# Turning 128x128 squares on TensorE as two half tiles that land in two PSUM banks

## The chip, the cores and the metric

The kernel runs on one core of a Trainium2 chip. The metric is the device time of one execution in microseconds (us). TensorE (PE in the profile) multiplies, VectorE (DVE), ScalarE (ACT) and GpSimd (POOL) do the elementwise work, SyncE (SP) issues the transfers. PE writes its results to PSUM, which has eight banks of 2 KB for each of 128 partitions (512 float32 numbers); the other engines read them from there.

## What is computed

One layer of a streaming encoder for one sequence of 1024 tokens of width 1024 in float32, with 16 meta tokens ahead of it. A mixer of two branches and an MLP, each with a normalization ahead and a residual around it:

```python
def hybrid_mixer(u, ...):                       # u = rmsnorm(h, norm_mix)
    z = u @ w_in                                # split into a, q, k, v, r, lr, ga, gb
    y_a = pooled(a) @ w_pool_mix ... @ w_pool_out
    o = gla_chunked(q, k, v, log_a)             # chunks of 64 tokens, 4 heads, keys 64 wide, values 128
    o = rmsnorm(o, gla_norm) * silu(r)
    y_b = o @ w_gla_out
    m = sigmoid(ga) * y_a + sigmoid(gb) * y_b
    return m @ w_out

h = h + hybrid_mixer(rmsnorm(h, norm_mix), ...)
h = h + squared_relu_mlp(rmsnorm(h, norm_ffn), w_ff1, w_ff2)
return rmsnorm(h, norm_final)[:, 16:]           # the meta tokens are dropped
```

Within a chunk, `gla_chunked` forms scores of queries and keys with a decay between them; across chunks it carries a state of 64x128 numbers for each head.

## The kernel before, in words

**Products.** A float32 product is made as three products of two-part numbers, hi times hi, lo times hi and hi times lo (`mm3`, lines 285 to 287). A step of `mm3` is three instructions of 128x128 weights that move up to 512 columns. ACT makes each hi part by rounding, DVE each lo part by subtracting. The projections and both MLP layers use seven products in place of eight on 2x2 blocks.

**Turning.** A product needs the contracted index on the partitions, so activations that stand token by token are turned. That is done on PE by `pe.transpose`: a 128x128 square of the activation is loaded as the weights, an identity matrix is moved through, and the turned square comes out in PSUM. Four squares fill a bank. The places are:

- line 525, `turn` of the first stage: eight tiles of 128 tokens of the normalized input (`us`), 8 squares each in a bank of the pool `ms` and one of `sc`. Its readers are `keep` (L531, ACT), `hi` (L538, ACT) and `lo` (L541, DVE);
- line 278: the 16 meta tokens, 8 pieces of 16x128;
- line 1417, in `across`, the part of the linear attention that carries the state: the keys `gi`, twice 8 squares, read by ACT (L1418);
- line 1461, later in `across`: the normalized output `on`, 32 squares, read by DVE (L1462);
- line 1589, `turn_tile`: the normalized input of the MLP (`u`), eight tiles of 8 squares. Six of them stand between the products of `out_tile` (the product with `w_out`, second half of its columns, `ch` = 1), two between the first products of the MLP's first layer, `ff1`. Readers are L1594, L221 and L222 for four of the tiles and L1598 to L1609 for the other four.

All in all 176 squares of 128x128, in 21 visits: 20 of 8 squares and one, in `across`, of 16. Ahead and behind of a visit stand ordinary products.

**Order.** PE's order is the program's own. In the first stage the orders of ACT, DVE and SP are written out as well (a list named ORDER_1). Elsewhere a scheduler orders ACT, DVE and SP by when it thinks that data are there. So a change of the PSUM pools can reorder DVE and ACT.

**PSUM.** The eight banks are split into pools by `banks(...)`, and the split changes from stage to stage: a product takes a bank of its pool when the earlier tenant has been read. `two(name)` takes a pair of neighbouring banks as one tile. In the linear attention before the change there are three `mm` banks for the products that fill in (`yb_block` among them, whose bank is read by L1388), one pair `m2`, one pair `sc` and one bank `ms`.

The tile positions of the profile read "64*64 64x64": a tile of 64 rows and 64 columns of the array that moves 64 columns. Such tiles exist before the change in `scores` (L1188), `across` (L1423, L1437, L1447).

Of the kernel before, what the change touches and what calls it, by code (L numbers as in the profile page):

```python
# [122 lines left out]
def kernel(  # L123
# [26 lines left out]
    banks(sc=1, mm=3, ms=3)  # L150
# [110 lines left out]
    turn_n = [0]  # L261

    def transposed(u, half, at, tags=("ms",), to=None):
        rows = u.shape[0]
        th, tl = (t[half] for t in to or (TH, TL))
        if rows == P:
            for j in range(2):
                turn_n[0] += 1
                b = bank(tags[turn_n[0] % len(tags)]).rearrange("p (a b) -> p a b", a=4)
                for i in range(4):  # L270
                    pe.transpose(b[:, i], u[:, (4 * j + i) * P : (4 * j + i + 1) * P], ident)
                split_from_psum(th[:, 4 * j : 4 * j + 4, at : at + P], tl[:, 4 * j : 4 * j + 4, at : at + P], b)
                c = half * HALF + at - OFF[half]
                act.activation(S["xr"][:, 4 * j : 4 * j + 4, c : c + P], b, ACT.Copy)
        else:
            b = bank("ms")[:, : 8 * rows].rearrange("p (a b) -> p a b", a=8)
            for i in range(8):
                pe.transpose(b[:, i], u[:, i * P : (i + 1) * P], ident[:rows, :rows])
            split_from_psum(th[:, :, at : at + rows], tl[:, :, at : at + rows], b)
# [165 lines left out]
    def first_stage(xs, us, xm, um, lrraw):  # L445
# [75 lines left out]
        def turn(t, j):  # L521
            turn_n[0] += 1
            b = turned[t, j] = bank(("ms", "sc")[turn_n[0] % 2]).rearrange("p (a b) -> p a b", a=4)
            for i in range(4):
                pe.transpose(b[:, i], x_out(t)[:, (4 * j + i) * P : (4 * j + i + 1) * P], ident)

        def kept(t, j):
            return xr[:, 4 * j : 4 * j + 4, t * P : (t + 1) * P]
# [4 lines left out]
        def part(a, t, j):  # L533
            half, at = tok(t)
            return a[half][:, 4 * j : 4 * j + 4, at : at + P]
# [640 lines left out]
    def part(i):  # L1176
        return slice(i * CH, (i + 1) * CH)

    def scores(kk, qq):
# [5 lines left out]
        for j in range(4):  # L1185
            for e, u in ((0, 0), (1, 1), (1, 0), (0, 1)):
# [93 lines left out]
    def gla_open():  # L1280
# [22 lines left out]
        banks(keep=1, mm=3, m2=1, ms=1)  # L1303
# [100 lines left out]
    def across(p, half):  # L1404
# [10 lines left out]
        b = quad(bank("ms") if p == 0 else wide2()[:, 0])  # L1415
        for j in range(4):
            pe.transpose(b[:, j], kl[:, j * P : (j + 1) * P], ident)
# [514 lines left out]
```

## Time and profile before

| | us |
|---|---|
| median of 3 runs (lowest to highest) | 1202.58 (1202.22 to 1203.32) |
| profiled execution | 1203.16 |
| its span, first to last instruction | 1201.4 |
| PE busy | 1187.1 |
| DVE busy | 854.1 |
| ACT busy | 578.7 |

The mean clock that TensorE was granted is 0.998. From 0 to about 60 us the span holds the first stage, to 180 the first products of the projections, to 380 the pairs of projections with the scores between them, to 480 the part of the linear attention that carries the state with the filling products, to 580 the product with `w_out`, and then the MLP.

A row of the timeline reads: start in us, duration in us, engine, line, operation, output<-inputs by the program's names, the tile of the array where it is a PE instruction, the moved form and the count of merged instructions, and in brackets the idle time ahead of it with what ended it. Durations of PE instructions overlap, since they are pipelined, so the pace is read from start to start. A row of the waits reads: the waiting engine, tile and line, `<-`, what ended the wait, and then the total in us, the count, and the longest.

### The profile page before, as it was taken

To read this page: it belongs to the slowest core of one execution; us is meant where nothing else is said; L and a number is where in the kernel's file an instruction comes from. 1 tells how busy PE (TensorE), PEld (TensorE's weight loads), DVE (VectorE), ACT (ScalarE), POOL (GpSimd) and SP (SyncE) were. 2 spreads that over 40 slices of the span, in tenths; PEclk is the share of its full clock that TensorE was granted. 3 is DMA by queue.
4 is the path that set the end of the run, shared out by engine and by line. 5 is a ranking of instruction groups with operands and counts; after the bars stand their busy time and mean duration, and the time that the engine had idled before them with its cause. 6 is when DMAs were issued, how large, how long until landed. Compare 5 with 4: busy or idle time off the path is not lost.

```text
span 1201.4 us, 18340 instructions
## 1 busy us (share of the span) xinstructions
PE 1187.1 (99%) x6775; PEld 987.7 (82%) x6775; DVE 854.1 (71%) x1392; ACT 578.7 (48%) x1006; POOL 101.5 (8%) x121
## 2 busy tenths in 40 slices
PE   9999999999999999999999999999999999999997
PEld 7999888777778887888788888888888888888886
DVE  6679557575676669617886767667675887887686
ACT  7566544444455224205754545545454444445554
POOL 0224232333220000000000000000000000000000
PEclk9999999999999999999999999999999999999999
DMA  8232633434358877801264444444389963333532
GB/s 246 68 89 80 182 109 119 144 117 141 124 178 269 304 229 269 268 26 71 88 198 136 158 147 162 148 158 161 128 282 324 336 222 97 97 97 92 172 97 88
DMA packets 151001, 192.79 MB, mean 160 GB/s; under 512 B 12088, under 2 KB 85616, under 8 KB 150912
## 3 DMA queue, kind: packets, MB, share of 16 engines
q1 hardware_dynamic: 150752, 191.56, 49.6%
q8 instruction: 53, 0.87, 0.3%
q14 instruction: 36, 0.29, 0.1%
q10 hardware_dynamic: 160, 0.07, 0.0%
HBM read 128.66 MB, written 62.93 MB: 159 GB/s over the span
## 4 chain that ended last, share of the span: by engine, by line
PE 68%; DVE 3%; issue 1%; DMA 1%; ACT 1%; SPq 0%; DVEq 0%
PE b_oa L287 5%; PE b_oa L286 5%; PE b_oa L285 5%; PE b_y L285 4%; PE b_y L287 4%; PE b_y L286 4%; PE b_mm L285 4%; PE b_mm L287 4%; PE b_mm L286 4%; PE b_ob L287 4%; PE b_ob L286 4%; PE b_ob L285 4%; PE b_z L286 3%; PE b_z L285 3%; PE b_z L287 3%; PE b_sc L285 2%
## 5 line engine op out<-in xcount | busy, mean ns | idle before, releaser
L285 PE MATMUL b_z<-th,w1h 128*128 128x512 f32 x240 | 94.3, 393 | 0.0
L286 PE MATMUL b_z<-tl,w1h 128*128 128x512 f32 x240 | 93.5, 390 | 0.4 <-DVE tl L1601 0.4
L287 PE MATMUL b_z<-th,w1l 128*128 128x512 f32 x240 | 93.5, 390 | 0.0
L285 PE MATMUL b_sc<-th,w1h 128*128 128x512 f32 (+1 forms) x232 | 89.8, 387 | 0.6 <-ACT u2p L1715 0.6
L286 PE MATMUL b_sc<-tl,w1h 128*128 128x512 f32 (+1 forms) x232 | 89.2, 385 | 0.0
L967 ACT ACTIVATE w1h<-raw 128x512 fp32r<-128x512 f32 x103 | 64.0, 622 | 52.4 <-PE b_y L286 23.0
L287 PE MATMUL b_sc<-th,w1l 128*128 128x512 f32 (+1 forms) x232 | 88.9, 383 | 0.0
L967 ACT ACTIVATE w1h<-fs 128x512 fp32r<-128x512 f32 x81 | 51.1, 631 | 66.3 <-PE b_y L286 34.8
L968 DVE TENSOR_TENSOR w1l<-raw,w1h 128x512 fp32r<-128x512 f32 x103 | 70.7, 688 | 15.7 <-ACT w1h L967 15.7
L968 DVE TENSOR_TENSOR w1l<-fs,w1h 128x512 fp32r<-128x512 f32 x81 | 56.2, 693 | 21.6 <-ACT w1h L967 21.6
L967 ACT ACTIVATE w1h<-bt 128x512 fp32r<-128x512 f32 x46 | 29.1, 632 | 70.9 <-issue 43.9
L1791 DVE TENSOR_TENSOR bt<-w,w 128x512 f32<-128x512 f32 x80 | 54.8, 684 | 1.1 <-DMA w<-in_w_ff_dram 1.1
L286 PEld LDWEIGHTS b_z<-tl,w1h 128*128 128x128 f32 x240 | 45.1, 188 | 9.9 <-DVE tl L1601 0.8
L285 PEld LDWEIGHTS b_z<-th,w1h 128*128 128x128 f32 x240 | 45.0, 188 | 9.8 <-issue 0.3
L287 PEld LDWEIGHTS b_z<-th,w1l 128*128 128x128 f32 x240 | 45.1, 188 | 9.7
L285 PEld LDWEIGHTS b_sc<-th,w1h 128*128 128x128 f32 x232 | 43.5, 188 | 10.3 <-ACT u2p L1715 1.1
L287 PEld LDWEIGHTS b_sc<-th,w1l 128*128 128x128 f32 x232 | 43.6, 188 | 8.9
L286 PEld LDWEIGHTS b_sc<-tl,w1h 128*128 128x128 f32 x232 | 43.6, 188 | 8.6
L285 PE MATMUL b_mm<-wo,th 128*128 128x512 f32 x128 | 50.4, 393 | 0.0
L968 DVE TENSOR_TENSOR w1l<-bt,w1h 128x512 fp32r<-128x512 f32 x46 | 31.8, 691 | 25.6 <-ACT w1h L967 25.6
L287 PE MATMUL b_mm<-wo,tl 128*128 128x512 f32 x128 | 49.9, 390 | 0.0
L286 PE MATMUL b_mm<-wo,th 128*128 128x512 f32 x128 | 49.8, 389 | 0.0
(526 smaller groups left out, 3416.3 us busy)
## 6 DMA issues: line engine op xcount, KB each, us to landing
hf_dram<-h SPq DMA_DIRECT2D x112, 256.0 KB, 2.1
raw<-hf_dram SPq DMA_DIRECT2D x112, 256.0 KB, 2.7
w<-in_w_ff_dram SPq DMA_DIRECT2D x64, 256.0 KB, 4.8
raw<-in_w_in_dram SPq DMA_DIRECT2D x18, 512.0 KB, 4.7
raw<-in_w_ff_dram SPq DMA_DIRECT2D x16, 512.0 KB, 4.3
rawx<-in_w_ff_dram SPq DMA_DIRECT2D x16, 512.0 KB, 4.1
rawp<-in_w_in_dram SPq DMA_DIRECT2D x14, 512.0 KB, 4.7
xs<-in_x_dram SPq DMA_DIRECT2D x8, 512.0 KB, 5.2
```

The costliest lines, as they stand in the source:

```text
L285: pe.matmul(ps, ah, bh, start=first and i == 0, stop=False, skip_group_check=more)
L286: pe.matmul(ps, ah, bl, start=False, stop=False, skip_group_check=more)
L287: pe.matmul(ps, al, bh, start=False, stop=last and i == n - 1, skip_group_check=more)
L967: act.activation(hi, a, ACT.Copy)
L968: dve.tensor_tensor(lo, a, f32(hi), ALU.subtract)
L1791: dve.tensor_tensor(bt, w, S["w2"][q[3:]][:, i], ALU.add if q[2] == "+" else ALU.subtract)
```

## The change

Each square is turned by two instructions in place of one. `turn_square` loads rows 0 to 63 of the square into the upper half of the array (64 rows by 128 columns) and rows 64 to 127 into the lower half, and moves a 64x64 identity through each. The upper half writes its 64 columns to bank 0 of a pair of banks, the lower half to bank 1. A turned square therefore lies half in one bank and half in the other, and each reader takes both by one access pattern of partition, square, bank and 64 numbers. The pieces of 16x128 of line 278 stay as they are.

```diff
-    banks(sc=1, mm=3, ms=3)
+    banks(sc=1, mm=3, ms=1, y2=1)
...
+    def turn_square(pair, k, a):
+
+        for u in range(2):
+            pe.transpose(pair[:, u, part(k)], a[part(u)], ident[part(u), part(u)], tile_position=(u * CH, 0))
+
+    def turned_view(pair, n):
+        return pair.rearrange("p u (k s) -> p k u s", s=CH)[:, n]
+
+    def four(a):
+        return a.rearrange("p k (u s) -> p k u s", s=CH)
...
         def turn(t, j):
-            turn_n[0] += 1
-            b = turned[t, j] = bank(("ms", "sc")[turn_n[0] % 2]).rearrange("p (a b) -> p a b", a=4)
-            for i in range(4):
-                pe.transpose(b[:, i], x_out(t)[:, (4 * j + i) * P : (4 * j + i + 1) * P], ident)
+            if j == 0:
+                turned[t] = two("y2" if t % 2 else "sc")
+            for k in range(4 * j, 4 * j + 4):
+                turn_square(turned[t], k, x_out(t)[:, k * P : (k + 1) * P])
+            turned[t, j] = turned_view(turned[t], slice(4 * j, 4 * j + 4))
...
-        banks(keep=1, mm=3, m2=1, ms=1)
+        banks(keep=1, mm=4, m2=1)
...
-        b = quad(bank("ms") if p == 0 else wide2()[:, 0])
+        b = wide2()
         for j in range(4):
-            pe.transpose(b[:, j], kl[:, j * P : (j + 1) * P], ident)
-        act.activation(kt, b, ACT.Copy)
+            turn_square(b, j, kl[:, j * P : (j + 1) * P])
+        act.activation(four(kt), turned_view(b, slice(0, 4)), ACT.Copy)
...
-        b = wide2().rearrange("p e (j c) -> p (e j) c", j=4)
+        b = wide2()
         for j in range(8):
-            pe.transpose(b[:, j], on[:, j], ident)
-        dve.tensor_tensor(sr, b.rearrange("p a c -> p (a c)"), sr, ALU.mult)
+            turn_square(b, j, on[:, j])
+        sr8 = four(sr.rearrange("p (a c) -> p a c", c=P))
+        dve.tensor_tensor(sr8, turned_view(b, slice(0, 8)), sr8, ALU.mult)
...
     def merge_open():
-        banks(keep=2, ms=3)
+        banks(keep=2, m2=1)
...
     def wo1_open():
         raw.back()
+        banks(keep=1, mm=2, m2=2)
...
-    def turn_tile(t, tags=("ms",)):
+    def turn_tile(t):
...
-        cols, b = slice(g * P, (g + 1) * P), []
+        cols, b, pair = slice(g * P, (g + 1) * P), [], two("m2")
         for j in range(2):
-            turn_n[0] += 1
-            b.append(quad(bank(tags[turn_n[0] % len(tags)])))
-            for i in range(4):
-                pe.transpose(b[j][:, i], u[:, (4 * j + i) * P : (4 * j + i + 1) * P], ident)
+            k = slice(4 * j, 4 * j + 4)
+            for i in range(4 * j, 4 * j + 4):
+                turn_square(pair, i, u[:, i * P : (i + 1) * P])
+            b.append(turned_view(pair, k))
```

The pools follow from it: the first stage has one `ms` bank and a second pair `y2`; the linear attention has four `mm` banks and no `ms`; the product with `w_out` has, in its second half, two `mm` banks and two pairs `m2`. Lines behind the new helpers stand some lines lower: 285 to 287 are now 290 to 292, 1388 is 1391, 1389 is 1392, 1393 is 1396, 1538 is 1542, 1599 to 1609 are 1603 to 1613, and all turns of squares are line 270.

**PE at the first turn of the keys** (before line 1417, where two banks take four squares each). Before:

```order
L286 MATMUL b_mm<-tl_136,w1h 128x512
L287 MATMUL b_mm<-th_132,w1l 128x512
L1417 MATMUL b_ms<-ident,gi_3849 128x128 x4
L1417 MATMUL b_sc<-ident,gi_3853 128x128 x4
L285 MATMUL b_mm<-th_132,w1h 128x512
```

With the change:

```order
L291 MATMUL b_mm<-tl_139,w1h 128x512
L292 MATMUL b_mm<-th_135,w1l 128x512
L270 MATMUL b_m_4017<-ident,gi_3913 128x64 x8
L270 MATMUL b_sc<-ident,gi_3917 128x64 x8
L290 MATMUL b_mm<-th_135,w1h 128x512
```

The neighbours stay, and eight instructions of 128 moved columns become sixteen of 64. It is the same at every other visit.

**DVE at the last `yb_block`s**, where L1388 (now L1391) reads the bank of a filling product, here with the number of each bank's tenant. Before:

```order
L1538 TENSOR_TENSOR wo0_4704<-acc_4708,wo0_4704 128x1024 x2
L85 TENSOR_TENSOR w1l_128<-raw0_116,w1h_124 128x1024
L1388 SCALAR_TENSOR_TENSOR o_4720<-o_4720,b_mm_4785 128x512
L1388 SCALAR_TENSOR_TENSOR t1_4716<-t1_4716,b_mm_4732 128x512
L1538 TENSOR_TENSOR wo0_4704<-acc_4708,wo0_4704 128x1024
L1389 TENSOR_TENSOR t1_4716<-t1_4716 128x512
```

With the change:

```order
L1542 TENSOR_TENSOR wo0_4812<-acc_4816,wo0_4812 128x1024 x2
L85 TENSOR_TENSOR w1l_131<-raw0_119,w1h_127 128x1024
L1391 SCALAR_TENSOR_TENSOR t1_4824<-t1_4824,b_mm_4840 128x512
L1542 TENSOR_TENSOR wo0_4812<-acc_4816,wo0_4812 128x1024
L1392 TENSOR_TENSOR t1_4824<-t1_4824 128x512
L1391 SCALAR_TENSOR_TENSOR t1_4824<-t1_4824,b_mm_4859 128x512
L1391 SCALAR_TENSOR_TENSOR o_4828<-o_4828,b_mm_4893 128x512
```

Tenant 4785 of before is tenant 4893 of the change: its reader stood first behind L85 and now stands two readers of L1391 later. Before, the next product (tenant 4804) was given the same bank as 4785. With four banks the product of the same place (tenant 4912) is given the bank of tenant 4771, whose reader stands ahead of all these rows.

**DVE at the opening of the MLP**, at the last `turn_tile` (`w1l`, `fs` and `t4l` belong to the MLP's weights and products, `tl` is the lo part of the turned tile). Before:

```order
L968 TENSOR_TENSOR w1l<-fs,w1h 128x512
L1599 TENSOR_TENSOR acc<-b_ms,acc 128x512
L222 TENSOR_TENSOR tl_144<-b_mm,th_140 128x4x128
L1603 TENSOR_TENSOR acc<-b_mm,acc 128x512
L1601 TENSOR_TENSOR tl_144<-acc,th_140 128x4x128
L1604 TENSOR_TENSOR acc<-b_mm,acc 128x512
```

With the change:

```order
L974 TENSOR_TENSOR w1l<-fs,w1h 128x512
L1603 TENSOR_TENSOR acc<-b_m_5791,acc 128x512
L1009 TENSOR_TENSOR fs<-fs,raw_119 128x512
L1673 TENSOR_TENSOR t4l<-acc,t4h 128x4x128
L1605 TENSOR_TENSOR tl_147<-acc,th_143 128x4x128
L222 TENSOR_TENSOR tl_147<-b_m_5791,th_143 128x4x128
```

L1601, now L1605, stays fifth, behind other company: two operations for the weights have come ahead of it, and the two that read the tile's second half have gone behind.

More of the change, by code (lines that the diff above doesn't have):

```diff
@@ L261, with part, transposed @@
     turn_n = [0]
-    def transposed(u, half, at, tags=("ms",), to=None):
+    QUARTERS = ((0, 0), (1, 1), (1, 0), (0, 1))
+    def part(i):
+        return slice(i * CH, (i + 1) * CH)
+    def turn_square(pair, k, a):
[5 more added lines that the diff above has]
+        return a.rearrange("p k (u s) -> p k u s", s=CH)
+    def transposed(u, half, at, to=None):
         rows = u.shape[0]
         th, tl = (t[half] for t in to or (TH, TL))
-        if rows == P:
-            for j in range(2):
-                turn_n[0] += 1
-                b = bank(tags[turn_n[0] % len(tags)]).rearrange("p (a b) -> p a b", a=4)
-                for i in range(4):
[L271 to L279, printed above, removed]
+        b = bank("ms")[:, : 8 * rows].rearrange("p (a b) -> p a b", a=8)
+        for i in range(8):
+            pe.transpose(b[:, i], u[:, i * P : (i + 1) * P], ident[:rows, :rows])
+        split_from_psum(th[:, :, at : at + rows], tl[:, :, at : at + rows], b)
     def mm3(ps, n, lhs, rhs, first=True, last=True, more=False):
@@ L534, in part @@
             half, at = tok(t)
-            return a[half][:, 4 * j : 4 * j + 4, at : at + P]
+            return four(a[half][:, 4 * j : 4 * j + 4, at : at + P])
         def hi(t, j):
@@ L1174, in meta_state @@
         yield 1.0
-    def part(i):
-        return slice(i * CH, (i + 1) * CH)
     def scores(kk, qq):
@@ L1185, in scores @@
         for j in range(4):
-            for e, u in ((0, 0), (1, 1), (1, 0), (0, 1)):
+            for e, u in QUARTERS:
                 r, to, s = part(e), part(u), part(2 * j + u)
@@ L1421, in across @@
         for j in range(4):
-            for u, e in ((0, 0), (1, 1), (1, 0), (0, 1)):
+            for u, e in QUARTERS:
                 pe.matmul(
@@ L1444, in across @@
         for j in (3, 0, 1, 2):
-            for e, u in ((0, 0), (1, 1), (1, 0), (0, 1)):
+            for e, u in QUARTERS:
                 c = 2 * j + u
@@ L1577, in out_tile @@
         return fn
[L1579 removed]
+    def turn_tile(t):
         u, acc, g = S["u2"][:, ORDER.index(t) % 2], S["acc"], t % 4
[L1584 removed]
+        cols, b, pair = slice(g * P, (g + 1) * P), [], two("m2")
         for j in range(2):
[L1586 to L1589 removed]
+            k = slice(4 * j, 4 * j + 4)
+            for i in range(4 * j, 4 * j + 4):
+                turn_square(pair, i, u[:, i * P : (i + 1) * P])
+            b.append(turned_view(pair, k))
+        at = lambda a, k=slice(0, 4): four(a[:, k, cols])
         lo, hi = (quad(acc[:, g, c]) for c in halves())
```

20 lines of the change are left out of this document (9 added, 11 removed).

## The prediction

> **What bounds the kernel now.** I read the page first: the busy time by engine.
>
> ```profile
> PE 1187.1 (99%) x6775; PEld 987.7 (82%) x6775; DVE 854.1 (71%) x1392; ACT 578.7 (48%) x1006; POOL 101.5 (8%) x121
> ```
>
> PE is busy for 1187.1 of 1201.4 us; 14.3 us are idle. So what shortens PE's own stream shortens the kernel, unless the saving runs into one of the few waits. The view of PE's waits names those that matter here:
>
> ```profile
> PE b_mm L285 <- DVE o L1388: 0.9, 1, 0.9
> PE b_sc L285 <- ACT u2p L1715: 0.6, 2, 0.4
> PE b_z L286 <- DVE tl L1601: 0.4, 1, 0.4
> ```
>
> The first is a full bank in the linear attention, the other two lie at the opening of the MLP. Then I read the timeline of PE around the turns, for two visits, of 8 and of 16 squares:
>
> ```profile
> 384.05 0.40 PE L287 MATMUL b_mm<-th,w1l 128*128 128x512 f32 x1
> 384.28 0.60 PE L1417 MATMUL b_ms<-ident,gi 128*128 128x128 f32 x4
> 384.72 0.60 PE L1417 MATMUL b_sc<-ident,gi 128*128 128x128 f32 x4
> 385.08 0.48 PE L285 MATMUL b_mm<-th,w1h 128*128 128x512 f32 x1
> 385.39 0.39 PE L286 MATMUL b_mm<-tl,w1h 128*128 128x512 f32 x1
> ```
>
> ```profile
> 414.21 0.39 PE L287 MATMUL b_mm<-th,w1l 128*128 128x512 f32 x1
> 414.44 1.03 PE L1461 MATMUL b_m<-ident,on 128*128 128x128 f32 x8
> 415.31 1.04 PE L1461 MATMUL b_sc<-ident,on 128*128 128x128 f32 x8
> 416.10 0.48 PE L285 MATMUL b_mm<-th,w1h 128*128 128x512 f32 x1
> 416.42 0.40 PE L286 MATMUL b_mm<-tl,w1h 128*128 128x512 f32 x1
> ```
>
> Groups of four follow at 0.44 us (384.28 to 384.72), of eight at 0.87: 0.109 a square. Ordinary products step by 0.227. What a visit costs is the time from the product ahead (384.05) to the second one behind (385.39) less two steps: 1.34 - 0.45 = 0.89 us for 8 squares, and 416.42 - 414.21 - 0.45 = 1.76 for 16. No switch of tile shape stands here, and nothing waits.
>
> **The price of the new visit.** No row shows a 64x128 half tile that turns. The nearest are the scores: four 64x64 tiles side by side, each moving 64 columns, with 32 instructions (8 groups of four) in one visit and 64 in another.
>
> ```profile
> 196.25 0.39 PE L287 MATMUL b_sc<-th,w1l 128*128 128x512 f32 x1
> 196.57 1.19 PE L1188 MATMUL b_gs<-n 64*64 64x64 f32 x64
> 197.69 0.50 PE L285 MATMUL b_y<-t1h,w1h 128*128 128x512 f32 x1
> 198.03 0.39 PE L286 MATMUL b_y<-t1l,w1h 128*128 128x512 f32 x1
> ```
>
> ```profile
> 351.83 0.71 PE L1188 MATMUL b_gs<-n 64*64 64x64 f32 x32 [0.15 <-DVE gi L1243]
> 352.47 0.50 PE L285 MATMUL b_y<-t1h,w1h 128*128 128x512 f32 x1
> ```
>
> From first score to next product it is 1.12 us for 16 groups (196.57 to 197.69) and 0.64 for 8 (351.83 to 352.47): 0.060 a group, plus a tail of 0.16. The entry costs 0.32 in place of 0.227 (196.25 to 196.57), the second product behind comes after 0.34 (197.69 to 198.03) in place of 0.227: 0.20 more. A visit of n groups costs 0.36 + 0.060n. A group loads 128 columns into each half of the rows and moves 64 columns through each; a pair of the change does the same in two instructions. Taking n as squares: 8 cost 0.84, 16 cost 1.32. Against 0.89 and 1.76 that is -0.05 and -0.44. The switch eats nearly all of the gain in a visit of 8, which breaks even at 0.066 a square.
>
> The bound below is the meta turn, with 128 columns loaded and only 16 moved:
>
> ```profile
> 55.63 0.29 PE L286 MATMUL b_mm<-vw,th 128*128 128x272 f32 x1
> 55.76 0.29 PE L287 MATMUL b_mm<-vw,tl 128*128 128x272 f32 x1
> 55.98 0.66 PE L278 MATMUL b_ms<-ident,um 16*128 16x16 f32 x8
> 56.58 0.39 PE L285 MATMUL b_mm<-vw,th 128*128 128x272 f32 x1
> 56.80 0.29 PE L286 MATMUL b_mm<-vw,th 128*128 128x272 f32 x1
> ```
>
> Its neighbours step by 0.13 (55.63 to 55.76), so it costs 56.80 - 55.76 - 0.25 = 0.79 for 8 squares: -0.10 a visit. The bound above is that the two halves run one after the other, each at the pace of a group: 0.12 a square, 1.32 and 2.28 a visit, +0.43 and +0.52. I take the scores, whose load and movement are those of a pair.
>
> Eight loads of 128 columns follow here within 0.60 us (55.98 to 56.58), at most 0.075 each. The Trainium skill ("TensorE: Matmul & The Clock Gate", section "LDWEIGHTS (loading the stationary operand)") says that a load takes its count of columns over 1.2 in ns, 107 ns for 128, whatever the rows; by it a pair could not pass under 0.107 us, a visit of 8 would be about 1.2 us (an estimate from that figure), and the change would lose time. The row of 0.075 disagrees with it.
>
> **The change part by part.**
>
> - *Linear attention.* Five visits: two of the keys, one of 16 squares, two of 8. 4 x -0.05 - 0.44 = -0.6. PE waits nowhere near them, so it shows in full.
> - *Between the products with `w_out`.* Six visits in a stretch without a wait: 6 x -0.05 = -0.3.
> - *Opening of the MLP.* Behind both last visits PE waits for ACT (the 0.6 above), and then for DVE's `tl` (0.4). A shorter turn only lengthens that wait. L1601 stays fifth in its piece of DVE's order, so `tl` comes as late as before: 0.
> - *First stage.* Eight visits, with other neighbours:
>
> ```profile
> 10.30 0.66 PE L525 MATMUL b_sc<-ident,us 128*128 128x128 f32 x4
> ...
> 11.64 1.99 PE L394 MATMUL b_mm<-raw,xr 128*128 128x256 f32 x8 [0.25 <-ACT xr L531]
> ...
> 17.74 0.66 PE L525 MATMUL b_sc<-ident,us 128*128 128x128 f32 x4
> ```
>
> ```profile
> 10.99 0.60 ACT L531 ACTIVATE xr<-b_sc 128x512 f32<-128x512 f32 x1 [1.59 <-PE b_sc L525]
> ```
>
>   ACT waits for the first four squares, and from there on works without a gap to the statistics (L494) of the tile that is turned at 17.74. Four squares at 0.060 instead of 0.109 let it start 0.2 earlier: -0.2 for all that follows. The second visit is hidden by the wait ahead of 17.74. The third starts from an idle PE, so it pays no entry and saves 0.1; the five behind it save 0.05 each. Together -0.5, between 0 and -0.9.
> - *The bank that was full.*
>
> ```profile
> 472.90 0.39 PE L287 MATMUL b_mm<-yg,w1l 128*128 128x512 f32 x1
> 474.17 0.50 PE L285 MATMUL b_mm<-yg,w1h 128*128 128x512 f32 x1 [0.88 <-DVE o L1388]
> 474.51 0.40 PE L286 MATMUL b_mm<-yg,w1h 128*128 128x512 f32 x1
> ```
>
> ```profile
> 465.63 0.68 DVE L1388 SCALAR_TENSOR_TENSOR o<-o,b_mm 128x512 f32<-128x512 f32 x1
> ...
> 473.43 0.68 DVE L1388 SCALAR_TENSOR_TENSOR o<-o,b_mm 128x512 f32<-128x512 f32 x1
> ```
>
>   The product due at 472.90 + 0.23 = 473.13 starts at 474.17, since its bank is read at 473.43, behind L85: 1.04 late, and 0.11 more on the restart (0.34 to the next). With four banks its tenant before is the one read at 465.63. The wait goes; I count -1.1. The bank of the reader that moved back two places is wanted again only three products later (36 steps of 0.227, 8 us). If another full bank takes the place, the term is between 0 and -1.1.
> - *Readers.* The access over two banks is priced by a reader that takes two banks today, against one that reads a bank straight:
>
> ```profile
> L1246 ACT ACTIVATE gi<-b_gs 128x512 f32<-128x512 f32 x4 | 2.4, 590 | 1.3 <-PE b_gs L1188 1.3
> L531 ACT ACTIVATE xr<-b_ms 128x512 f32<-128x512 f32 x8 | 4.8, 599 | 0.0
> ```
>
>   590 ns against 599: nothing. For DVE I have no such row and take nothing too; PE is the bound and covers it, except at the MLP's opening, where 10 reads at 5% (30 ns of some 0.6 us) would make 0.3.
>
> Sum: -0.6 - 0.3 - 0.5 - 1.1 = -2.5 us. The profiled execution of 1203.16 would become 1200.7, the span 1198.9. The runs' median is 0.58 below that execution, so the forecast for the median is 1202.58 - 2.5 = **1200.1**. The changes that a measurement here can tell from none begin at 0.2%, 2.4 us: the forecast lies on that line.
>
> **The rivals.**
>
> - *More than forecast.* The pair has the meta turn's price, 0.79 a visit: eleven visits of the attention and of `w_out` gain, ten of them 0.10 and the big one 0.48 (0.79 and 8 more squares at 0.06, 1.28), together -1.5, the first stage -0.9, the bank -1.1: -3.5, 1199.1. For it speaks that no more than two tiles are in use at a time; against it, that 16 moved columns are fewer than 64.
> - *Less: the stall moves.* The visits gain as forecast, but the bank is replaced by another wait, or the first stage gives its part to its next wait. -0.6 - 0.3 - 0.2 = -1.1, 1201.5. For it: DVE's order there is changed, and L85 still stands ahead of the readers. Against it: the new product's bank is read 7.5 us ahead.
> - *Slower: the halves of a pair don't run beside each other.* It decides at every visit from 0.066 us a square upward. At 0.12 ten visits of 8 lose 0.43, the big one 0.52, six of the first stage 0.43, the two at the opening 0.2 (part goes into the wait there): 4.3 + 0.5 + 2.6 + 0.2 - 1.1 = +6.5, 1209. At the pace of today's whole square, 0.109, it is 0.34 at each of the 17 visits and 0.1 at the opening: 5.8 + 0.1 - 1.1 = +4.8, 1207. For it: both halves fill all 128 columns of the array, which the four score tiles do only between them. Against it: the scores' 0.060 could not come out if rows and columns had to take turns. The rule of the Trainium skill named above, of a load by its columns, would make it this second case, 1207; the row of 0.075 is why the two together get no more than a tenth.
> - *Slower: the opening of the MLP.* Two operations more ahead of `tl` or slower reads make PE wait there 2 us longer and eat the rest: 1202 to 1203. Against it: fifth stays fifth.
>
> **Chances.** Forecast 0.55 (its own range 1199.4 to 1200.9: 0.3 of the 0.55 under the line of 1200.17, 0.25 above it); more 0.14; less, or the opening eating the gain, 0.20; slower through the halves 0.11. Faster 0.3 + 0.14 = 0.44; same 0.25 + 0.2 = 0.45, less 0.01 for an opening that goes past +2.4 us; slower 0.12. The range takes the forecast, both neighbours and a small loss: 1198.4 to 1204.0, with the halves left out above and a little below.
>
> **What would show it.** Right: line 270 at the second visits steps 0.06 a pair, and a visit of 8 costs 0.84, of 16 1.32, measured as above; the wait on L1391 at about 472 us is gone from PE's waits; ACT's first `xr` copy starts at 10.75. Wrong: a pair at 0.1 us or more; a new wait of PE for DVE in the attention or at the opening; ACT's or DVE's reads over two banks longer than 0.60 and 0.69 us for 512 numbers.

## The result, and the profile after

The change made the kernel slower.

| | before | change |
|---|---|---|
| median of 4 runs each, us (lowest to highest) | 1202.95 (1202.22 to 1203.79) | 1212.22 (1209.48 to 1213.35) |
| ratio (95% interval) | | 1.0072 (1.0060 to 1.0085) |
| profiled execution, us | 1203.16 | 1211.22 |
| its span | 1201.4 | 1209.2 |

The page of the change, busy time by engine, in us with the share of the span and the count of instructions:

```profile
PE 1187.5 (98%) x6951; PEld 981.3 (81%) x6951; DVE 854.4 (71%) x1392; ACT 578.1 (48%) x1006; POOL 101.4 (8%) x121
```

PE is as busy as before (1187.5 against 1187.1), though it runs 176 instructions more. Of the 7.8 us that came on top of the span, 7.4 are idle time of PE, and the view of PE's waits names where (tile, line, what ended the wait: total, count, longest):

```profile
PE b_mm L290 <- DVE acc L1577: 3.0, 1, 3.0
PE b_z L290 <- ACT wo L1612: 2.5, 1, 2.5
...
PE b_mm L290 <- ACT vo L416: 0.8, 1, 0.8
PE b_mm L399 <- ACT xr L537: 0.7, 1, 0.7
```

The full bank of the linear attention, 0.9 before, has left the list. Shown are four of the waits that are new or have grown. To see what each is worth, set the start of the same product of PE in the two profiled executions side by side:

| product | before | change | change is later by |
|---|---|---|---|
| last of the first stage's waits | 64.10 | 67.06 | 2.96 |
| ahead of the visit of 16 squares | 414.21 | 417.40 | 3.19 |
| behind that visit | 416.10 | 418.87 | 2.77 |
| the one that found its bank full | 474.17 | 475.89 | 1.72 |
| third tile of `out_tile`, first half | 498.82 | 503.60 | 4.78 |
| first of the MLP's `b_z` | 594.33 | 602.16 | 7.83 |
| the next one | 595.14 | 602.47 | 7.33 |
| last product | 1193.26 | 1200.87 | 7.61 |

So there are three losses: about 3 us in the first stage, 3.1 in the product with `w_out`, 2.7 at the opening of the MLP (of which 0.5 comes back). Two turns late in the product with `w_out` lose 0.3 each besides. And there are the two gains that were forecast for the linear attention, 0.4 and 1.05.

The gains first. The timeline of PE in the change, rows as explained with the profile before; the two visits and then the full bank:

```profile
387.27 0.39 PE L292 MATMUL b_mm<-th,w1l 128*128 128x512 f32 x1
387.59 0.46 PE L270 MATMUL b_m<-ident,gi 64*128 64x64 f32 x8
387.88 0.42 PE L270 MATMUL b_sc<-ident,gi 64*128 64x64 f32 x8
388.23 0.50 PE L290 MATMUL b_mm<-th,w1h 128*128 128x512 f32 x1
388.57 0.40 PE L291 MATMUL b_mm<-tl,w1h 128*128 128x512 f32 x1
...
417.40 0.39 PE L292 MATMUL b_mm<-th,w1l 128*128 128x512 f32 x1
417.72 0.71 PE L270 MATMUL b_m<-ident,on 64*128 64x64 f32 x16
418.27 0.67 PE L270 MATMUL b_sc<-ident,on 64*128 64x64 f32 x16
418.87 0.50 PE L290 MATMUL b_mm<-th,w1h 128*128 128x512 f32 x1
419.21 0.40 PE L291 MATMUL b_mm<-tl,w1h 128*128 128x512 f32 x1
...
475.66 0.39 PE L292 MATMUL b_mm<-yg,w1l 128*128 128x512 f32 x1
475.89 0.39 PE L290 MATMUL b_mm<-yg,w1h 128*128 128x512 f32 x1
```

Eight squares (sixteen instructions of 64x128 tiles) follow at 0.55 us (417.72 to 418.27), 0.069 a square against 0.109 before. With the entry of 0.32 and the 0.34 behind, a visit of 8 costs 388.57 - 387.27 - 0.45 = 0.85, one of 16 costs 419.21 - 417.40 - 0.45 = 1.36. The product that stood idle at 474.17 now follows its forerunner at 0.23.

Now the two long waits, in the timeline of PE and then of DVE:

```profile
500.24 0.39 PE L292 MATMUL b_mm<-wo,tl 128*128 128x512 f32 x1
503.60 0.50 PE L290 MATMUL b_mm<-wo,th 128*128 128x512 f32 x1 [2.97 <-DVE acc L1577]
...
599.25 0.39 PE L292 MATMUL b_sc<-th,w1l 128*128 128x512 f32 x1
602.16 0.47 PE L290 MATMUL b_z<-th,w1h 128*128 128x512 f32 x1 [2.53 <-ACT wo L1612]
602.47 0.40 PE L291 MATMUL b_z<-tl,w1h 128*128 128x512 f32 x1
```

```profile
500.58 2.36 DVE L1542 TENSOR_TENSOR wo<-raw,wo 128x1024 fp32r<-128x1024 f32 x2 [1.18 <-ACT wo L1541]
502.86 0.68 DVE L1577 TENSOR_TENSOR acc<-b_mm,acc 128x512 f32<-128x512 f32 x1
...
601.34 0.68 DVE L1608 TENSOR_TENSOR acc<-b_m,acc 128x512 f32<-128x512 f32 x1
```

At 500.47 the third tile of `out_tile` was due. It starts at 503.60, when DVE has read an earlier tile (L1577, 502.86 to 503.54); that read stands behind two operations of L1542 that split a weight. At 599.48 `b_z` was due. It starts at 602.16, just after the last read of the pair that was turned last (L1608, 601.34 to 602.02). The view of waits puts that down to ACT's L1612, the first of which ended at about the same time; in the program as built the product waits for L1608. Both products are the first to want a bank of a *new* pool: `wo1_open` now splits the banks anew (`banks(keep=1, mm=2, m2=2)`), and the MLP's `z` lies on the banks 6 and 7, in which the change keeps a pair `m2`. In the program as built, the third tile of `out_tile` lies in bank 2, and the read that it waits for is of a tile in bank 5. So the first tiles of a new pool wait for the readers of all the pools that it replaces, and not only for those of their own bank. The third tile belongs to the first half of the columns: the split into two `mm` banks and two pairs is there from this tile on, and not only in the second half, as the section on the change has it.

The first stage, in the timelines of ACT and DVE at one of its tiles, ACT first:

```profile
31.09 0.60 ACT L544 ACTIVATE th<-b_sc 128x512 fp32r<-128x512 f32 x1 [0.54 <-PE b_sc L270]
33.57 0.60 ACT L544 ACTIVATE th<-b_sc 128x512 fp32r<-128x512 f32 x1 [1.88 <-DVE tl L547]
```

```profile
32.85 0.68 DVE L547 TENSOR_TENSOR tl<-b_sc,th 128x512 fp32r<-128x512 f32 x1
34.20 0.69 DVE L547 TENSOR_TENSOR tl<-b_sc,th 128x512 fp32r<-128x512 f32 x1 [0.67 <-ACT th L544]
```

Before, the same four reads were of two single banks:

```profile
29.14 0.60 ACT L538 ACTIVATE th<-b_sc 128x512 fp32r<-128x512 f32 x1
29.63 0.59 ACT L538 ACTIVATE th<-b_ms 128x512 fp32r<-128x512 f32 x1
```

```profile
31.04 0.68 DVE L541 TENSOR_TENSOR tl<-b_sc,th 128x512 fp32r<-128x512 f32 x1
31.64 0.68 DVE L541 TENSOR_TENSOR tl<-b_ms,th 128x512 fp32r<-128x512 f32 x1
```

Before, ACT read both halves of the tile back to back, long before DVE. Now ACT's second read waits 1.88 us until DVE's first one has ended, and DVE's second waits 0.67 for ACT's second: the pair is taken in turns. The groups of ACT up to 70 us (busy time and mean ns; idle time ahead and what ended it) show how much of it there is:

```profile
L544 ACT ACTIVATE th<-b_y 128x512 fp32r<-128x512 f32 x8 | 4.8, 594 | 2.7 <-DVE tl L547 2.7
...
L544 ACT ACTIVATE th<-b_sc 128x512 fp32r<-128x512 f32 x6 | 3.6, 598 | 3.9 <-DVE tl L547 2.6 <-PE b_sc L270 1.3
```

Before, the same groups waited for DVE nowhere (the `xr` copies did, 1.0 in all; now it is 0.3). And the first copy of the stage waits for eight squares in place of four. The timelines of PE and of ACT in the change:

```profile
11.44 0.71 PE L270 MATMUL b_sc<-ident,us 64*128 64x64 f32 x16
```

```profile
12.19 1.08 ACT L537 ACTIVATE xr<-b_sc 128x512 f32<-128x512 f32 x2 [2.90 <-PE b_sc L270]
```

It starts 0.75 after the first turn, where it was 0.69 before (10.30 to 10.99).

How much of the 2.96 belongs to the stage is told by the other runs' traces, if the start of the kernel, whose pace varies (last section), is left out. From the first warm-up product behind the small products of the start to the product at 64.10 it is 56.7 us before, and between 56.2 and 56.7 in all five executions that have this first stage. It is 58.9 in all four that have the change's (the change twice, b_mm and c_z below). So the stage itself loses some 2.3, and the small products 0.7.

The Trainium skill ("PSUM — Partial Sum Buffer", section "PSUM bank collisions raise a hardware error") says that two engines must not touch one bank at the same partitions at the same time, reads against reads included, and that they have to be kept apart. The order that the trace shows agrees with it; no run here shows a collision itself. By that rule each half of a tile, now spread over both banks, excludes the other engine from both. But the turns are taken also where the two halves lie in different banks (p_pair_whole below), so it is already the pair as one tile that makes them.

### The profile page after: what moved, and what is told of

Same layout as the page of the kernel before. It is cut to its first block, busy times and chain, and to the rows that moved or that the text cites. A ratio compares the mean times of both kernels' runs of the same rounds, so it can differ in the third digit from the quotient of the medians.

```text
span 1209.2 us, 18684 instructions
## 1 busy us (share of the span) xinstructions
PE 1187.5 (98%) x6951; PEld 981.3 (81%) x6951; DVE 854.4 (71%) x1392; ACT 578.1 (48%) x1006; POOL 101.4 (8%) x121
## 4 chain that ended last, share of the span: by engine, by line
PE 62%; DVE 5%; DMA 3%; issue 2%; ACT 1%; SPq 0%; DVEq 0%; ACTq 0%
PE b_oa L292 5%; PE b_oa L290 5%; PE b_oa L291 5%; PE b_y L290 4%; PE b_y L291 4%; PE b_y L292 4%; PE b_ob L292 4%; PE b_ob L290 4%; PE b_ob L291 4%; PE b_mm L290 3%; PE b_mm L291 3%; PE b_mm L292 3%; PE b_z L290 3%; PE b_z L291 3%; PE b_z L292 3%; PE b_sc L290 2%
```

## The experiments

The theory at first: the halves do what was forecast, and the loss lies in what came with them, the new splits of the banks, the first stage's pairs, and its `ms` pool of one bank. The rival: the halves, or the reads over two banks, are dear by themselves. Results of all, each against runs of the kernel before on its own chip (where medians of two chips are compared below, the kernel before tells how far the chips differ: 1202.38 to 1202.95):

| kernel | median, us (range) | before | ratio (95%) |
|---|---|---|---|
| a_warm | 1214.17 (1211.95 to 1216.11) | 1202.44 | 1.0097 (1.0081 to 1.0112) |
| b_mm | 1208.22 (1207.88 to 1209.66) | 1202.44 | 1.0050 (1.0035 to 1.0065) |
| c_z | 1210.40 (1208.48 to 1211.83) | 1202.44 | 1.0065 (1.0050 to 1.0080) |
| e_whole | 1214.07 (1212.96 to 1214.75) | 1202.44 | 1.0098 (1.0081 to 1.0115) |
| d_pools | 1205.61 (1204.85 to 1205.91) | 1202.38 | 1.0025 (1.0015 to 1.0036) |
| g_first | 1202.68 (1202.08 to 1202.99) | 1202.38 | 1.0002 (0.9992 to 1.0011) |
| h_whole | 1203.65 (1203.30 to 1204.15) | 1202.38 | 1.0012 (1.0003 to 1.0021) |
| m_gla | 1200.81 (1200.14 to 1201.83) | 1202.38 | 0.9985 (0.9976 to 0.9993) |
| n_gla_whole | 1201.42 (1200.39 to 1202.55) | 1202.67 | 0.9989 (0.9980 to 0.9998) |
| p_pair_whole | 1204.37 (1203.61 to 1205.28) | 1202.67 | 1.0015 (1.0006 to 1.0024) |
| q_pair_half | 1203.56 (1202.73 to 1205.30) | 1202.67 | 1.0009 (1.0000 to 1.0018) |
| r_change | 1209.61 (one run) | 1202.67 | |

**a_warm: the change, with one bank for each group of warm-ups.** The change leaves the first stage one bank `ms`, and each warm-up product asks for it anew.

```diff
         def warm(n, cols=HALF):
+            b = bank("ms")[:, :cols]
             for _ in range(n):
-                pe.matmul(bank("ms")[:, :cols], blank[:, HALF:], blank[:, :cols], start=True, stop=True)
+                pe.matmul(b, blank[:, HALF:], blank[:, :cols], start=True, stop=True)
```

> The change, with one edit: the warm-up products of the first stage take their PSUM bank once for each group of products instead of once for each product, so that a product no longer waits for the one before it on the single ms bank. Theory (banks): the change is slow because its pools make PE wait, and the first of these waits is the warm-up: in the changed kernel the products that spread the norm weights ran at 0.213 us instead of 0.112 until 7.1 us, gB came at 7.43 instead of 6.74, and the later warm-up products stepped by 0.53 to 0.65 instead of 0.43. With the edit gB comes at about 6.75, the first turn starts at 10.3 to 10.5 instead of 11.44, and the time falls by 0.9 to 1.2 us against the change (about 1211 us where the change has 1212.2). Rival (halves): the half tiles themselves cost the time, in the array or in their readers; then the start of the first turn may move, but the end stays within 0.3 us of the change.

The gain did not show. The median is above that of the change, in a range of 4 us, and its product at 64.10 of before starts at 67.04, where the change's starts at 67.06. The warm-ups themselves closed up (the one at 10.38 in the change starts at 10.02), but in this execution the small products that follow the first warm-ups (last section) reached their full pace only at 7.5 us, and TensorE ran at 0.50 of its clock for some 3 us behind the wait for `b_z` (as in the next experiment). So the medians don't show the effect of this edit. The traces do: counted as above, from behind the small products to the product at 64.10 of before, it is 58.7 us in the three executions that have this edit and half tiles (a_warm, d_pools, q_pair_half), and 58.9 without it. It is worth 0.2.

**b_mm: the change without the new split at `wo1_open`.**

```diff
         raw.back()
-        banks(keep=1, mm=2, m2=2)
```

> The change without its new split of PSUM at the second half of w_out: the four mm banks and the one pair m2 of the linear attention stay. Theory (banks): the first product of the newly opened mm pool waits for the readers of every tile of the pools it replaces, the wait of 3.0 us on L1577 near 500 us. Without the split this wait is gone and the time falls by 2.7 to 3.3 us against the change (about 1209 where the change has 1212.2); a new wait of up to 0.5 us may come at the last turn, since there is one pair instead of two. Rival (halves): the wait belongs to the longer way of DVE, and something else holds the product as long; the time falls by less than 1 us.

1208.22, 4.0 below the change's median, and 3.5 when each is set against the kernel before on its own chip, a little more than expected. The 3.0 us wait is gone: in the timeline of PE the third tile follows its forerunner at 0.22.

```profile
499.48 0.39 PE L292 MATMUL b_mm<-wo,tl 128*128 128x512 f32 x1
499.70 0.39 PE L290 MATMUL b_mm<-wo,th 128*128 128x512 f32 x1
```

The other one stays (view of PE's waits):

```profile
PE b_z L290 <- ACT wo L1611: 2.5, 1, 2.5
```

So the split at `wo1_open` makes the first long wait, as the theory has it. What comes behind the second wait was new. The windows of PE in b_mm (stretch, its length, busy time and instructions of PE, weight loads, DVE, ACT, POOL; granted clock; then the DMA's share and GB/s):

```profile
598.00:600.00 2.00, 1.83 (x7) 1.56 (x8) 2.00 (x5) 1.28 (x3) 0.00 (x0) 0.90 0.00 0
600.00:602.00 2.00, 2.00 (x6) 1.60 (x5) 1.63 (x3) 0.00 (x0) 0.00 (x0) 0.50 0.00 0
602.00:604.00 2.00, 2.00 (x8) 1.55 (x8) 1.30 (x3) 1.97 (x4) 0.00 (x0) 0.74 0.00 0
```

After the wait of 2.5 us TensorE runs at 0.50 of its clock for some 3 us, and the stretch ends 1.2 us later than it would have.

**c_z: the change, with the MLP's `z` on other banks.**

```diff
-        banks(keep=1, y=4, z=2)
+        banks(keep=1, z=2, y=4)
```

> The change, with the banks of the MLP's first layer laid out the other way round: z on banks 2 and 3, y on banks 4 to 7, so that the first product into z doesn't take a bank of the last turned pair. Theory (banks): the first b_z product no longer waits 2.5 us for the last reader of the pair; it waits for tl (L1605) as in the kernel before, about 0.4 us. The time falls by 1.8 to 2.6 us against the change. The first y product, which now takes the pair's banks, comes 5.4 us later and waits for nothing new. Rival (DVE's order): DVE simply comes later with tl in its new order, and the wait at the first b_z products stays over 1.5 us.

The wait at the opening goes, as expected: `b_z` starts 2.7 us earlier against the products around it. But 300 us later another one opens, since the last product layer's pool `oa` now lies over `z`. PE's waits in c_z:

```profile
PE b_mm L290 <- DVE acc L1577: 2.3, 1, 2.3
PE b_oa L290 <- DVE h L1747: 1.8, 1, 1.8
```

And here it is the first of the two long waits that is followed by half the clock (501.00 to 503.00 is the end of the wait; same columns as above):

```profile
501.00:503.00 2.00, 0.50 (x1) 0.50 (x2) 2.00 (x3) 0.42 (x1) 0.00 (x0) 0.88 0.48 156
503.00:505.00 2.00, 2.00 (x6) 1.52 (x5) 0.57 (x1) 0.00 (x0) 0.00 (x0) 0.50 1.06 316
505.00:507.00 2.00, 2.00 (x8) 1.59 (x8) 1.00 (x2) 1.15 (x2) 0.00 (x0) 0.77 1.09 335
```

It costs 1.6 us beyond the wait. Of the gain of 2.7 no more than 1.8 is left in the medians, 1210.40 against 1212.22 (1.3 when each is set against its own kernel before). So a wait that a pool's place makes was moved, not removed.

**e_whole: the change, with whole squares into the same pairs.** The turn is one instruction of 128x128 again, four squares to a bank; splits of the banks and order of the program stay those of the change.

```diff
-        for u in range(2):
-            pe.transpose(pair[:, u, part(k)], a[part(u)], ident[part(u), part(u)], tile_position=(u * CH, 0))
+        pe.transpose(pair[:, k // 4, (k % 4) * P : (k % 4 + 1) * P], a, ident)
...
-        return pair.rearrange("p u (k s) -> p k u s", s=CH)[:, n]
+        return pair.rearrange("p e (k u s) -> p (e k) u s", k=4, s=CH)[:, n]
```

> The change with whole squares: every square is turned by one transpose of 128x128 into one bank of the same pair, as before, in the pools and with the order of the change. Only the cutting in halves is undone. Theory (banks): the halves gain what was forecast (0.04 us in a visit of 8, 0.41 in the one of 16, against 847 and 1354 ns measured), the pools lose; so this kernel is slower than the change by 0.6 to 1.2 us, about 1213. Readers of one bank may start after the first four squares again, which could give 0.2 us back at each of a few turns of the first stage. Rival (halves): the halves cost the time; then this kernel comes back to 1203 to 1205.

1214.07, 1.9 above the change (2.4 when each is set against its own kernel before), more than expected, on the side expected. In the profiled execution 1.3 of it stands in the first stage: 60.3 us, counted as above, in place of 58.9. The halves are not the cause, nor are reads that step to and fro between two banks, which this kernel doesn't have. The rival falls.

**d_pools: the change with the pools opened once.** The pair lies on banks 2 and 3, four `mm` banks on 4 to 7, from the linear attention on; no new split at the two places behind it; and the warm-ups of a_warm.

```diff
-        banks(keep=1, mm=4, m2=1)
+        banks(keep=1, m2=1, mm=4)
...
     def merge_open():
-        banks(keep=2, m2=1)
...
     def wo1_open():
         raw.back()
-        banks(keep=1, mm=2, m2=2)
```

> The change with half tiles everywhere, but no new split of PSUM after the linear attention: four mm banks on 4 to 7 and one pair m2 on 2 and 3, opened once and kept until the MLP, so that neither the first product of w_out's second half nor the first b_z product takes a bank of tiles that are still being read; and the warm-up of the first stage without its waits. Theory (pools): both long waits of PE (3.0 on L1577, 2.5 at b_z) are gone, and with them the stretches at half clock that follow such waits in some executions. Left are the first stage (+1.5 to +2.2 us, its readers wait for whole pairs), against -0.4 for the halves in the attention, -1.1 for the bank that was full, -0.2 at w_out, and +0.5 for turns that wait for their input: 1202.5 to 1204, and the spread of the executions falls from 4 us to 2 or less. Rival (readers): DVE's and ACT's later order at the opening of the MLP holds PE there by itself, also without the pool; then 1205 or more.

1205.61. Both long waits are gone, and with them most of the spread: 7 runs lie within 1.06 us, where 4 of the change lie over 3.9. It is above the range expected for it. In number that is the rival's 1205 or more, in kind it is not: at the opening PE waits for DVE's `tl` alone, 0.4 as before. The reason is of the same kind as the waits that went. `mm` now lies on the banks in which the stage ahead keeps `b_z`, and its first product waits for the read of that (next experiment). The product that starts at 377.48 before is 1.11 later than those ahead of it.

**g_first and h_whole: d_pools with the first stage of before (whole squares in single banks), and the same with whole squares everywhere.** The edit of g_first puts back the split `banks(sc=1, mm=3, ms=3)`, `turn`, its views and the warm-ups; h_whole adds the edit of e_whole.

```diff
-    banks(sc=1, mm=3, ms=1, y2=1)
+    banks(sc=1, mm=3, ms=3)
...
-            for k in range(4 * j, 4 * j + 4):
-                turn_square(turned[t], k, x_out(t)[:, k * P : (k + 1) * P])
+            b = turned[t, j] = bank(("ms", "sc")[turn_n[0] % 2]).rearrange("p (a b) -> p a b", a=4)
+            for i in range(4):
+                pe.transpose(b[:, i], x_out(t)[:, (4 * j + i) * P : (4 * j + i + 1) * P], ident)
```

> As d_pools, but with the first stage of the kernel before: whole squares in banks of ms and sc, three ms banks. Theory (pools and pairs): the first stage's loss of some 2 us goes, the rest stays: 0.4 + 1.1 + 0.2 - 0.5 below the kernel before, 1201 to 1201.8. Rival (halves change the later stages too): it stays above 1202.5.

> As g_first with whole squares also in the attention and at w_out: same pools, same pairs, one transpose of 128x128 for each square. Against g_first it tells what the halves alone are worth where nothing else hides it: +0.4 for the visit of 16, +0.04 for each of ten visits of 8, so 0.6 to 0.8 us slower than g_first. If the halves were worth nothing or cost time, it is as fast as g_first or faster.

g_first is 2.9 below d_pools in the medians (2.4 in the first stage of the two profiled executions, counted as above): that is the price of the first stage's pairs. But it misses what was expected, and lies just above the 1202.5 of the rival. It still has the new wait. PE and then DVE in its timeline:

```profile
376.84 0.39 PE L292 MATMUL b_z<-th,w1l 128*128 128x512 f32 x1
378.18 0.47 PE L290 MATMUL b_mm<-th,w1h 128*128 128x512 f32 x1 [0.96 <-ACT w1h L84]
```

```profile
377.35 0.68 DVE L1106 TENSOR_TENSOR c<-b_z,u2p 128x512 f32<-128x512 f32 x1
```

The product starts at 378.18 in place of 377.07, after DVE's read of `b_z` has ended at 378.03; the program as built has it wait for that read, and the name in brackets, ACT's, is again only the neighbour. Without that 1.1, g_first would be at about 1201.6, inside what was expected. h_whole is 0.97 above g_first, a little more than expected: the halves by themselves, in the linear attention, between the products with `w_out` and at the MLP's opening, are worth one us.

**m_gla and n_gla_whole: the kernel before, with the pair and four `mm` banks in the linear attention alone, as halves and as whole squares.** First stage, `w_out` and MLP stay as before.

```diff
-        banks(keep=1, mm=3, m2=1, ms=1)
+        banks(keep=1, mm=4, m2=1)
...
-        b = quad(bank("ms") if p == 0 else wide2()[:, 0])
+        b = wide2()
         for j in range(4):
-            pe.transpose(b[:, j], kl[:, j * P : (j + 1) * P], ident)
-        act.activation(kt, b, ACT.Copy)
+            turn_square(b, j, kl[:, j * P : (j + 1) * P])
+        act.activation(four(kt), turned_view(b, slice(0, 4)), ACT.Copy)
...
     def merge_open():
-        banks(keep=2, ms=3)
+        banks(keep=2, ms=2)
```

> The kernel before, with half tiles in the linear attention alone, and there four mm banks; the first stage and the turns at w_out and at the MLP's opening are as before (whole squares in single banks, here two ms banks that take the place of the pair m2). Theory: -0.45 for the halves (five visits), -1.1 for the bank that was full, nothing lost: 1.5 us below the kernel before, about 1201.0, and below the change and all its variants. Rival: a new wait takes the bank's part, then only -0.4.

> As m_gla (four mm banks in the linear attention, everything else as before), with whole squares there: no half tile is left. It parts the two gains of m_gla (1200.81). Theory: the bank that was full gives -1.1 alone, so this kernel is at 1201.3 (0.4 to 0.6 above m_gla, 1.0 to 1.2 below the kernel before). Rival: the halves free PE's way in the attention and the bank gives nothing by itself; then it is as slow as before, 1202.4.

m_gla is the best of all: 1200.81, ratio 0.9985 with an interval that excludes 1, so it beats the kernel before by 1.6 us and the change by some 11. The bank is free when its product is due (472.20 follows 471.98, in the timeline of PE):

```profile
471.98 0.39 PE L292 MATMUL b_mm<-yg,w1l 128*128 128x512 f32 x1
472.20 0.39 PE L290 MATMUL b_mm<-yg,w1h 128*128 128x512 f32 x1
```

Set beside the kernel before as in the first table, it gains 0.41 at the visit of 16 and 1.06 from there to the product that found its bank full, 1.47 of the 1.6. n_gla_whole gains 1.05 at the bank alone, and stands 0.1% under its before. The two differ by 0.0004 in the ratio, which their intervals do not tell apart. So the fourth `mm` bank is the larger part, and it needs no halves.

**p_pair_whole and q_pair_half: m_gla with the change's pairs in the first stage, as whole squares and as halves.** Both have the warm-ups of a_warm.

```diff
-    banks(sc=1, mm=3, ms=3)
+    banks(sc=1, mm=3, ms=1, y2=1)
...
-            b = turned[t, j] = bank(("ms", "sc")[turn_n[0] % 2]).rearrange("p (a b) -> p a b", a=4)
+            if j == 0:
+                turned[t] = two("y2" if t % 2 else "sc")
             for i in range(4):
-                pe.transpose(b[:, i], x_out(t)[:, (4 * j + i) * P : (4 * j + i + 1) * P], ident)
+                k = 4 * j + i
+                pe.transpose(turned[t][:, j, i * P : (i + 1) * P], x_out(t)[:, k * P : (k + 1) * P], ident)
```

> As m_gla, with the first stage turning whole squares, but into the pairs of the change: one pair of banks for each tile of 128 tokens, four squares in each bank, pools sc, y2 and one ms bank, the warm-up without its waits. No half tile in the first stage, so what it loses against m_gla is the price of the pair as one unit that its readers wait for. Theory (pairs): +2.0 to +2.9 us against m_gla, 1203 to 1203.7, and ACT's first copy waits for all eight squares. Rival (halves): the pair costs nothing and the halves do; then 1201.

> As p_pair_whole with half tiles in the first stage, as the change has them. Theory (pairs): 0.4 to 0.7 us faster than p_pair_whole, since each visit ends earlier and the pair is free earlier: +1.5 to +2.2 against m_gla, 1202.4 to 1203. Rival (halves): slower than p_pair_whole.

p_pair_whole is 3.6 above m_gla (3.3 when each is set against its own kernel before), a little over what was expected, although each square lies in one bank, as before. Its timelines of PE and ACT:

```profile
10.67 1.09 PE L532 MATMUL b_sc<-ident,us 128*128 128x128 f32 x8
```

```profile
11.80 1.09 ACT L539 ACTIVATE xr<-b_sc 128x512 f32<-128x512 f32 x2 [2.63 <-PE b_sc L532]
```

ACT's first copy starts 1.13 after the first turn, once all eight squares are there; before, it was 0.69 (10.30 to 10.99), after four. And the `th` copies wait for DVE's `tl` as in the change, although the two reads are of different banks here. So it is enough that the two halves of a tile are one tile of the program: its readers wait for the whole of it, and for one another. The halves win a part back (0.8 us, q_pair_half), since eight of their squares come nearly as fast as four whole ones did (ACT's first copy starts 0.75 after the first turn). Against m_gla, each set against its own kernel before, q_pair_half loses 2.5, more than the 1.5 to 2.2 expected.

**r_change: the change once more.** It was to show whether the change's spread of 4 us is the clock behind its two waits.

> The changed kernel itself, unaltered, for a second profiled execution. Its executions lie between 1209.5 and 1213.4, 4 us apart, the kernel before's within 2. Theory (clock): the two long waits of PE, 3.0 and 2.5 us, are followed by a stretch at half clock in some executions and not in others; in the first profile neither was. Here the waits are found at the same places with the same length within 0.8 us, and any difference of more than 1 us in the span to the first profile's 1209.2 is found as granted clock under 1 in the stretches of 2 us behind the waits. Rival (transfers): the span differs because a transfer lands later, and the waits differ in length.

PE's waits stand where they stood:

```profile
PE b_mm L290 <- DVE acc L1577: 2.8, 1, 2.8
PE b_z L290 <- ACT wo L1612: 2.5, 1, 2.5
```

1209.61, 1.6 below the change's first profiled execution, and neither of the two has half a clock behind its waits. The 1.6 come from the start (0.6, the small products), from 0.4 between the first stage and the visit of 16 squares, and from tenths. So the clock does not explain this difference. It may explain the rest of the spread: the two slowest runs of the change, 1213.22 and 1213.35, had a mean granted clock of 0.995, the other two 0.998, and 0.003 of 1210 us is 3.6 us. But no trace of those two runs shows where.

## Why the prediction was wrong

The forecast was -2.5 us with a range of 1198.4 to 1204.0; it came to +9.3 in the medians. Step by step:

- *The price of the new visit*: right. 0.85 and 1.36 measured, 0.84 and 1.32 predicted; 0.069 a square in place of 0.060. The rival that the halves of a pair don't run beside each other is out, and with it the rule of the Trainium skill that the prediction weighed ("TensorE: Matmul & The Clock Gate", section "LDWEIGHTS (loading the stationary operand)"): two loads of 128 columns passed in 0.069 us, where it would give 0.107 for each.
- *Linear attention*, -0.6: the visit of 16 gave 0.40 (0.42 up to the first product behind it), the four of 8 gave 0.04 to 0.05 each. Right.
- *The bank that was full*, -1.1: right, 1.04 at the product itself in the change and in m_gla, and 0.1 on the restart. m_gla is these two terms alone: forecast -1.7, measured -1.6.
- *Readers*, nothing: right as far as their length goes. ACT's `xr` and `th` copies took 594 to 598 ns on average in the first stage, against 591 to 599 before, and DVE's `tl`, for which the prediction had no row, 688 and 690 against 682 and 688. Wrong in what was asked: it was priced how long a read over two banks takes, and not which other reads it excludes.
- *First stage*, -0.5, with a worst case of 0: measured +2.96 at 67 us, of which 0.7 is the pace of the small products at the start, which varies between executions, 0.2 the warm-ups on their one bank, and some 2.1 the pairs. This is the step "Four squares at 0.060 instead of 0.109 let it start 0.2 earlier" (0.2 off 10.99 would be 10.79, not the 10.75 that it names as a sign). The pairs end that: the first copy waits for eight squares and starts 0.06 later against the first turn, and the readers take turns. Priced by itself, d_pools against g_first, it is 2.9 us in the medians.
- *Between the products with `w_out`*, -0.3, "six visits in a stretch without a wait": four of the visits gave 0.04 each, but the new split at `wo1_open` put a wait of 3.0 into the first half of that product, some 47 us ahead of the first of them (3.2 with the restart). The diff showed the split; the prediction gave it no term. Two of the visits also wait 0.3 each for the normalization's statistics on DVE, and lose 0.30 each on balance. These waits stand in all traces of kernels that turn into pairs there (the change, d_pools and g_first among them), and in none of those that turn into single banks (m_gla, n_gla_whole, p_pair_whole, q_pair_half). In the change ACT reads the pair once more ahead of the statistics (L221 at 563.95, L251 at 564.43), where the statistics came first before; that this is the cause was not tried.
- *Opening of the MLP*, 0: measured +2.7 and -0.5. The prediction followed the order of DVE (`tl` as fifth) and not the banks: `b_z` waits for the last read of the pair, and `tl` (L1605, 599.54 to 600.22) was long there. The rival that named this place had it right, by another mechanism: its price, 2 us, is near the 2.2 measured here, and its 1202 to 1203 fell short because the other two places were not in it.

The three last are one omission. The prediction counted the instructions of the visits, and not the tenants of the banks: for none of the new splits did it ask which reads have to be over when the first product of the new pool is due, and for the pairs it did not ask which readers now share a tile.

The sizes can be put together from the medians, each set against the kernel before on its own chip. m_gla has the gains, -1.6. The pairs of the first stage cost 2.9 (d_pools over g_first). For the long waits stands d_pools, 6.0 below the change, and another 1.1 lower but for its own new wait, with the warm-ups' edit in it: 7.1. The pairs at the later places cost 0.8 (g_first but for its new wait, 1201.6, over m_gla); of that the traces show 0.4 in the turns with `w_out`. These four steps lead from the kernel before to the change by way of three kernels, so their sum gives the 9.3 by itself; what the runs tell is the sizes. The two long waits with their restarts account for 5.3 of the 7.1 in the profiled execution. The rest, 1.8, holds the 0.2 of the warm-ups and is not settled beyond them: half clock behind the waits, in some executions, is of that size, but the change's own two traces don't show it.

## What to carry to other kernels

A new layout in PSUM is priced by its tenants as well as by the instructions that fill it: for each split of the banks that a change adds or moves, find the first product of each new pool, and ask which reads of the old pools must be over then, and where these stand in their engine's order. Two banks taken as one tile tie their readers together; where two engines read the halves of a tile, two single banks let them run apart. And a gain per instruction is best taken where the layout is already there: the linear attention, which had its pair, kept all of the gain, and the first stage lost 2.9 us for 0.8.

## What of the hardware was not expected

After a wait of PE of 1.8 to 2.5 us the granted clock fell to about half for some 3 us in four profiled executions (a_warm, b_mm, c_z, e_whole, behind one of their two long waits each), and stayed at 1.00 behind waits of 2.5 to 3.0 in others (both traces of the change), so that a wait of the same kind costs between its own length and 1.6 us more. The Trainium skill ("TensorE: Matmul & The Clock Gate", section "What's actually happening") has the clock fall after an idle window of about 3.4 us, and has that window run freely. Shorter idle times than that, 1.8 to 2.5 us, were followed by half clock here, and not every time. A window that runs freely would fit the second, not the first by itself, and no run here tests it.

At the start of the kernel sixteen small products ran at half pace for a time that differs from execution to execution. The timeline of PE before, and then of the change:

```profile
5.58 2.02 PE L487 MATMUL b_mm<-us,ident 128*128 128x128 f32 x16 [0.33 <-DMA us<-in_norm_mix_dram]
```

```profile
5.48 2.80 PE L492 MATMUL b_mm<-us,ident 128*128 128x128 f32 x16
```

They began within 0.1 us of each other and took 0.8 us longer in the change, which doesn't touch them. The second execution of the change (r_change) had the next product at 7.49, the first at 8.12, the kernel before at 7.43. The view's granted clock is 1.00 there (5 to 8 us, before and change), so it doesn't tell the cause. Differences of that size in single profiled executions are not the edit's.
